# Two thirds of the attention probabilities transposed by VectorE and two trips through memory instead of by TensorE

## The chip, the cores and the metric

The kernel runs on one core of one Trainium2 chip. The metric is the device time of one execution in microseconds (us); the lower, the better.

## What is computed

A decoder trunk of two layers in fp32, for one sequence of 256 tokens with 1024 channels. Each layer adds half a SwiGLU FFN (inner width 2816), a mixer, and half of another FFN to the stream, each behind an RMSNorm; a last RMSNorm ends it.

```python
for layer in range(DEPTH):
    h = h + 0.5 * swiglu(rms_norm(h, ffn1_norm[layer]), ...)
    hn = rms_norm(h, mix_norm[layer])
    h = h + (ab_mixer(hn, ...) if layer % 2 == 0 else c_mixer(hn, ...))
    h = h + 0.5 * swiglu(rms_norm(h, ffn2_norm[layer]), ...)
return rms_norm(h, final_norm)
```

The mixer of layer 0 (ab) has eight causal attention heads of 64 channels under a fixed mask with weights, beside four groups of a spatial gate that mixes positions by a causal 128x128 matrix. The mixer of layer 1 (c) has 16 heads of 64 channels; at 256 tokens and blocks of 256 its block-sparse attention is plain causal attention. So in both, a head is softmax(q k^T + mask) v over 256 queries and 256 keys. The change concerns one step of that: for the product with v the softmax's probabilities, computed with the queries on the partitions, are needed with the keys on the partitions.

## The kernel before

**fp32 as three passes.** Each product of fp32 matrices is done as three matmuls in the format fp32r (`mm3`, L265 to L268): high part by high part, high by low, low by high. An operand is split by a ScalarE (ACT) copy to fp32r, which is the high part, and a VectorE (DVE) subtraction, which gives the low part (`split`, L271).

**The stream of weights.** The weights come as chunks of up to 1 MB by SyncE's (SP's) DMA queue into three raw buffers (L139, `Stream`), and are split into four buffers each of high and low parts (`whi` by ACT at L172, `wlo` by DVE at L173). `pump` loads and splits ahead as buffers come free; TensorE (PE) consumes the chunks in a fixed order. `hold` and `release` keep splits back around some steps of the ab mixer; `release` places them behind given instructions.

**Phases.** ffn, ab_mixer, ffn, ffn, c_mixer, ffn. In a mixer the projections to q, k and v (and to the gate's u and its norm in ab) run tile by tile: a tile of 128 output channels is 24 matmuls of 256 columns, half a block of v 12 of 512 columns. Each such piece is a step, and after it `Slots.step` emits the attention's pieces that are registered for this step number. The output projection, `project`, consumes `mix`, a pair of heads at a time, and has steps as well.

**A head's pieces.** `scores` makes the raw scores on PE (L700, L701), the masked minimum on DVE (L704), the exponential on ACT (L707), the reciprocal of the sum on DVE (L710) and the scaling on GpSimd (POOL; for the last heads on DVE, L714). The result is `pr`: 128 query partitions by 384 columns, since of the first 128 queries only 128 keys count. `turn` transposes it in three 128x128 blocks on PE (L723) into a PSUM bank and splits that into `pth` and `ptl` (L271). `weighted` multiplies a pair of heads with v (three matmuls of 512 columns and three of 256) and splits the result into `mixh` and `mixl`. `put_q`, `put_k` and `put_v` evict the projections' tiles (L659 to L685, L820, L821), `mixing` is the spatial gate (L859 to L868).

**Order.** Each engine executes its instructions in one fixed order, written at build time: a scheduler sorts the emitted instructions, and `tc.issue_after(x)` keeps what is emitted under it behind instruction x. Waits between engines are semaphores.

Of the kernel before, what the change touches and what calls it, by code (L numbers as in the profile page):

```python
# [10 lines left out]
F32 = mybir.dt.float32  # L11
# [4 lines left out]
S = 256  # L16
# [19 lines left out]
LINE, SHIFT = 64, 16  # L36
EDGE, GAP = 56, 240

# [76 lines left out]
class Stream:  # L115
# [31 lines left out]
    def split_parts(self):  # L147
        j = self.split
        nc = self.nc
        nk, w, _, shift, cuts, reset = self.specs[j]  # L150
        raw = self.raws.pop(j)
        his, los = (p.tile([128, CH + LINE], F32R, name=m) for p, m in ((self.hi_pool, "whi"), (self.lo_pool, "wlo")))

        h = w // 2
        far = nk * w - reset * h + RESHIFT // LINE * LINE + RESHIFT

        def at(k):
            return int(k * w) - reset * h + shift

        def part(t, k):  # L160
            if k >= reset:
                return t[:, at(k) : at(k) + w]
            return Halves(*(t[:, a : a + h] for a in (far + k * h, shift + k * h)))

        self.parts[j] = tuple([part(t, k) for k in range(nk)] for t in (his, los))

        def split(a, r):
            n = r.free_size()
            hi, lo = his[:, a : a + n], los[:, a : a + n]
            if len(r.shape) == 3:  # L170
                hi, lo = (t.rearrange("p (k c) -> p k c", k=reset) for t in (hi, lo))
            nc.scalar.activation(hi, r, AF.Copy)  # L172
            nc.vector.tensor_sub(lo, r, hi.bitcast(F32))  # L173
# [51 lines left out]
def trunk(ctx: ExitStack, tc: tile.TileContext, a, out):  # L225
# [419 lines left out]
    def make_attention(mp, mask_cols, nheads, v, mix, rows=False):  # L645

        qs, ks, probs, pts = {}, {}, {}, {}
        pairs, flying = (4, 5) if rows else (2, 4)
        seconds = [mp.tile([128, 2 * S + LINE], F32R, name=f"ql{i}") for i in range(pairs)]
# [7 lines left out]
        def scaled(bk):  # L657
            t = mp.tile([128, S], F32, name="qk", bufs=3)
            nc.vector.tensor_mul(t, bk[:, :S], norm["row"])  # L659
            return t  # L660
# [30 lines left out]
        def scores(h):  # L691
            q, ql = qs.pop(h)
            k = ks.pop(h)
            sc = bank()
            pr = mp.tile([128, 384], F32, name="pr", bufs=flying)
            nm = wk.tile([128, 2], F32, name="nm")
# [12 lines left out]
            rl = wk.tile([128, 2], F32, name="rl")  # L709
            nc.vector.reciprocal(rl, l)  # L710
            for b, (c0, n) in enumerate(((0, 128), (128, 256))):
# [27 lines left out]
        return put_q, put_k, scores, turn, weighted  # L739

# [83 lines left out]
    def ab_mixer(phase):  # L824
        with tc.tile_pool(name="mp", bufs=1) as mp:
# [3 lines left out]
            uT = mp.tile([128, 4, S], F32, name="uT")  # L829
            put_q, put_k, scores, turn, weighted = make_attention(mp, slice(0, 384), 8, v, mix)  # L830

# [63 lines left out]
    def c_mixer(phase):  # L895
        with tc.tile_pool(name="mp", bufs=1) as mp:
            mix = mix_tiles(mp)
            v = v_tiles(mp, D)
            put_q, put_k, scores, turn, weighted = make_attention(mp, slice(384, 768), 16, v, mix, True)
# [90 lines left out]
```

## Time and profile before

| what | value |
|---|---|
| median of 3 runs | 937.71 us |
| the three runs | 937.48, 937.71, 942.17 us |
| profiled execution | 937.01 us |
| its span on the core | 935.3 us |
| PE busy in the span | 927.7 us (99%) |
| DVE busy | 612.1 us (65%) |
| ACT busy | 499.2 us (53%) |
| POOL busy | 83.0 us (9%) |
| HBM | 173.72 MB read, 2.10 MB written |

The span is the part of the execution that the profile covers from its first to its last instruction. A row of a group reads: line, engine, operation, out<-in with shapes, count, then busy us and mean ns of one, then the engine's idle time just before and what ended it. In a timeline the first two numbers are the start in us from the span's start and the duration in us; the duration of a PE matmul contains a pipeline latency, so the distance from start to start is its cost. A row of a stretch (window) has the busy time of PE, PE's weight loads, DVE, ACT and POOL, with counts, then the granted clock, the share of the DMA engines and the GB/s. A row of DMA issues has size and median us from issue to landing.

### The profile page before, as it was taken

What the parts mean: (1) busy time and instruction counts of PE and PEld (TensorE: products, weight loads), DVE (VectorE), ACT (ScalarE), POOL (GpSimd) and SP (SyncE); (2) the same over time, 40 slices, a digit from 0 to 9 for tenths busy, and PEclk for the clock granted to TensorE, in tenths of its full rate; (3) what the DMA queues carried; (4) which work ended last, traced back from release to release, by engine and by line L of the source; (5) the groups of instructions that cost most, each with busy time, mean ns of one, the idle gap of its engine ahead of it and who ended that gap; (6) DMA issues with size and microseconds to landing.
All of it is one profiled execution on the core that took longest, in us unless ns stands there. A gap on an engine that the chain in (4) does not pass through costs nothing.

```text
span 935.3 us, 18101 instructions
## 1 busy us (share of the span) xinstructions
PE 927.7 (99%) x7655; PEld 907.4 (97%) x7655; DVE 612.1 (65%) x892; ACT 499.2 (53%) x782; POOL 83.0 (9%) x114
## 2 busy tenths in 40 slices
PE   9999999999999999999999999999999999999997
PEld 9999999999999999999999999999999999999886
DVE  7866556676888666555756665567787786656543
ACT  7744444468667454444454544456786665445431
POOL 0000000034210000000000000002574000000000
PEclk9999999999999999999999999999999999999999
DMA  8755554665336555555555555556543377555521
GB/s 320 281 212 181 189 194 162 223 222 180 136 136 226 188 211 188 183 175 206 204 184 200 204 180 170 203 184 220 177 139 136 137 243 269 186 188 210 190 90 46
DMA packets 28305, 176.99 MB, mean 189 GB/s; under 512 B 3264, under 2 KB 4672, under 8 KB 9152
## 3 DMA queue, kind: packets, MB, share of 16 engines
q1 hardware_dynamic: 26928, 173.65, 52.5%
q10 hardware_dynamic: 1296, 2.18, 0.7%
q8 instruction: 60, 0.98, 0.4%
q14 instruction: 21, 0.17, 0.0%
HBM read 173.72 MB, written 2.10 MB: 188 GB/s over the span
## 4 chain that ended last, share of the span: by engine, by line
PE 98%; issue 1%; DMA 0%; ACT 0%; SPq 0%; DVE 0%; POOLq 0%; POOL 0%
PE bank L266 30%; PE bank L267 30%; PE bank L268 30%; PE bank L567 2%; PE bank L571 2%; PE bank L568 2%; PE bank L723 1%; PE bank L700 1%; PE bank L701 1%; DMA x<-in_x 0%; PE bank L343 0%; PE bank L859 0%; PE bank L361 0%; PE bank L455 0%; PE bank L456 0%
## 5 line engine op out<-in xcount | busy, mean ns | idle before, releaser
L172 ACT ACTIVATE whi<-raw 128x1024 fp32r<-128x1024 f32 (+3 forms) x352 | 330.5, 985 | 350.1 <-issue 282.9
L173 DVE TENSOR_TENSOR wlo<-raw,whi 128x1024 fp32r<-128x1024 f32 (+3 forms) x352 | 389.6, 1141 | 126.7 <-ACT whi L172 125.8
L266 PE MATMUL bank<-xTh,whi 128*128 128x256 f32 x1616 | 447.9, 277 | 0.0
L267 PE MATMUL bank<-xTl,whi 128*128 128x256 f32 x1616 | 446.7, 276 | 0.0
L268 PE MATMUL bank<-xTh,wlo 128*128 128x256 f32 x1616 | 446.6, 276 | 0.0
L267 PEld LDWEIGHTS bank<-xTl,whi 128*128 128x128 f32 x1616 | 303.5, 188 | 0.2
L266 PEld LDWEIGHTS bank<-xTh,whi 128*128 128x128 f32 x1616 | 303.5, 188 | 0.0
L268 PEld LDWEIGHTS bank<-xTh,wlo 128*128 128x128 f32 x1616 | 303.5, 188 | 0.0
L267 PE MATMUL bank<-hTl,whi 128*128 128x256 f32 x528 | 145.8, 276 | 0.0
L266 PE MATMUL bank<-hTh,whi 128*128 128x256 f32 x528 | 145.8, 276 | 0.0
L268 PE MATMUL bank<-hTh,wlo 128*128 128x256 f32 x528 | 145.8, 276 | 0.0
L266 PEld LDWEIGHTS bank<-hTh,whi 128*128 128x128 f32 x528 | 99.1, 188 | 0.0
L268 PEld LDWEIGHTS bank<-hTh,wlo 128*128 128x128 f32 x528 | 99.1, 188 | 0.0
L267 PEld LDWEIGHTS bank<-hTl,whi 128*128 128x128 f32 x528 | 99.1, 188 | 0.0
L506 DVE TENSOR_TENSOR hm<-gs,bank 128x512 f32<-128x512 f32 x44 | 30.1, 687 | 77.7 <-PE bank L268 77.3
L503 DVE TENSOR_TENSOR gs<-bank,row 128x512 f32<-128x512 f32 x44 | 30.0, 689 | 47.8 <-PE bank L268 47.8
L266 PE MATMUL bank<-mixh,whi 128*128 128x256 f32 x128 | 35.3, 281 | 0.0
L267 PE MATMUL bank<-mixl,whi 128*128 128x256 f32 x128 | 35.1, 277 | 0.0
L268 PE MATMUL bank<-mixh,wlo 128*128 128x256 f32 x128 | 35.0, 277 | 0.0
L714 POOL TENSOR_SCALAR pr<-pr,rl 128x128 f32<-128x128 f32 (+1 forms) x36 | 30.8, 870 | 25.2 <-DVE rl L710 14.1
L653 POOL MEMSET ql<- 64x256 f32 x12 | 3.7, 307 | 328.7 <-ACT whi L172 170.3
L567 PE MATMUL bank<-whi,hTh 128*128 128x512 f32 x80 | 31.1, 389 | 0.0
(134 smaller groups left out, 877.4 us busy)
## 6 DMA issues: line engine op xcount, KB each, us to landing
raw<-in_weights SPq DMA_DIRECT2D x149, 1024.0 KB, 4.9
raw<-in_weights SPq DMA_DIRECT2D x12, 768.0 KB, 4.4
raw<-in_weights SPq DMA_DIRECT2D x6, 512.0 KB, 6.5
x<-in_x SPq DMA_DIRECT2D x4, 264.0 KB, 4.0
raw<-in_weights SPq DMA_DIRECT2D x4, 256.0 KB, 4.3
away<-xn SPq DMA_DIRECT2D x2, 512.0 KB, 5.5
xr<-away SPq DMA_DIRECT2D x8, 128.0 KB, 5.7
fg<-in_final_norm ACTq DMA_DIRECT2D x1, 512.0 KB, 3.7
```

The costliest lines, as they stand in the source:

```text
L172: nc.scalar.activation(hi, r, AF.Copy)
L173: nc.vector.tensor_sub(lo, r, hi.bitcast(F32))
L266: nc.tensor.matmul(p, sh, mh, start=start, stop=False)
L267: nc.tensor.matmul(p, sh, ml, start=False, stop=False)
L268: nc.tensor.matmul(p, sl, mh, start=False, stop=stop)
L503: nc.vector.tensor_mul(g, both(pg), twice(norm["row"]))
L506: nc.vector.tensor_mul(hm, g, both(pu))
L567: nc.tensor.matmul(banks[t, h], sh, w[0][kw][:, cs], start=k == 0, stop=False)
L568: nc.tensor.matmul(banks[t, h], sh, w[1][kw][:, cs], start=False, stop=False)
L571: nc.tensor.matmul(banks[t, h], sl, w[0][kw][:, cs], start=False, stop=k == FT - 1)
L700: nc.tensor.matmul(sc[:, b * S : (b + 1) * S], q[:, bs], k, start=True, stop=False)
L714: share = engine.tensor_scalar(pr[:, cs], pr[:, cs], rl[:, b : b + 1], None, op0=ALU.mult)
```

## The change

For the first four of the eight heads of ab and the first twelve of the sixteen of c, in groups of four, the transposition leaves PE. `tilt`, two steps behind the scores, transposes `pr` (128x384) on DVE in blocks of 32x32 into `turned`; it stands behind the latest reciprocal, or for the fourth head of a group behind the latest weight split. `send` writes the group to memory by four DMAs on SP, one for each 32 partitions; `fetch` reads it back by four more into `ptl`, with the blocks where the full transpose has them. `part` then splits: two ACT copies of 128x768 from `ptl` to `pth`, and two DVE subtractions in place; it is issued behind the latest weight split on both engines. `weighted` of these heads stands in later slots. The last four heads of each mixer go on as before, by `turn` on PE, though `pr` lies in `turned`.

`pth` and `ptl` now hold four heads in one buffer each, with the heads' columns interleaved in 32s, so `weighted` reads its moving operand in runs of 64 elements and `mix` is written accordingly. `pr` goes from 4 (ab) and 5 (c) buffers to 3, `qk` from 3 to 2, and the padding `GAP` from 240 to 112 elements. In c four of the sixteen scores stand one step earlier.

```diff
-EDGE, GAP = 56, 240
+EDGE, GAP = 56, 112
...
-            nc.scalar.activation(hi, r, AF.Copy)
-            nc.vector.tensor_sub(lo, r, hi.bitcast(F32))
+            self.last = nc.scalar.activation(hi, r, AF.Copy), nc.vector.tensor_sub(lo, r, hi.bitcast(F32))
...
-        qs, ks, probs, pts = {}, {}, {}, {}
-        pairs, flying = (4, 5) if rows else (2, 4)
+        qs, ks, probs, pts, sent = {}, {}, {}, {}, {}
+        pairs = 4 if rows else 2
+        late = nheads - 4
         seconds = [mp.tile([128, 2 * S + LINE], F32R, name=f"ql{i}") for i in range(pairs)]
...
-            t = mp.tile([128, S], F32, name="qk", bufs=3)
+            t = mp.tile([128, S], F32, name="qk", bufs=2)
...
-            pr = mp.tile([128, 384], F32, name="pr", bufs=flying)
+            if h < late:
+                pr = mp.tile([128, 384], F32, name="pr", bufs=3)
+            else:
+                if h == late:
+                    probs["turned"] = turned_tile()
+                pr = probs["turned"].rearrange("p m j h r -> p (m j h r)")[:, h % 4 * 384 : (h % 4 + 1) * 384]
...
-            nc.vector.reciprocal(rl, l)
+            probs["behind"] = nc.vector.reciprocal(rl, l)
...
+        def turned_tile():
+            return mp.tile([128, 3, 4, 4, 32], F32, name="turned")
+
+        def tilt(h):
+
+            if h % 4 == 0:
+                probs["turned"] = turned_tile()
+            turned = probs["turned"]
+            behind = st.last[1] if h % 4 == 3 else probs["behind"]
+            with tc.issue_after(behind.ins):
+                nc.vector.transpose(turned[:, :, :, h % 4].rearrange("p m j r -> p (m j) r"),
+                                    probs.pop(h).rearrange("p (b c) -> p b c", c=32))
+
+        def send(g):
+            sent[g] = dram.tile([32, 12, 4, 128], F32, name=f"sent{nheads}{g}")
+            for i in range(4):
+                nc.sync.dma_start(sent[g][:, :, i],
+                                  probs["turned"][i * 32 : (i + 1) * 32].rearrange("c m j h r -> c (m j) (h r)"))
+
+        def fetch(g):
+
+            src = sent.pop(g).rearrange("c (m j) i f -> j c m (i f)", j=4)
+            pts[g] = parts = part_tiles()
+            for j in range(4):
+                nc.sync.dma_start(parts[1][j * 32 : (j + 1) * 32].bitcast(F32).rearrange("p (m i) h r -> p m (i h r)", m=3),
+                                  src[j])
+
+        def part(g):
+
+            with tc.issue_after(st.last[0].ins), tc.issue_after(st.last[1].ins):
+                for q in range(2):
+                    hi, lo = (t[:, q * 6 : (q + 1) * 6] for t in pts[g])
+                    nc.scalar.activation(hi, lo.bitcast(F32), AF.Copy)
+                    nc.vector.tensor_sub(lo, lo.bitcast(F32), hi.bitcast(F32))
+
+        def part_tiles():
+
+            return [mp.tile([128, 12, 4, 32], F32R, name=n) for n in ("pth", "ptl")]
+
         def turn(h):
-            p, j = divmod(h, 2)
+            g, j = divmod(h, 4)
             pr = probs.pop(h)
             tp = bank()
             for i in range(3):
                 nc.tensor.transpose(tp[:, i * 128 : (i + 1) * 128], pr[:, i * 128 : (i + 1) * 128], ident)
             if j == 0:
-                pts[p] = [mp.tile([128, 2, 384], F32R, name=n, bufs=2) for n in ("pth", "ptl")]
-            return split(pts[p][0][:, j, :], pts[p][1][:, j, :], tp[:, :384])
+                pts[g] = part_tiles()
+            return split(*(t[:, :, j] for t in pts[g]), tp[:, :384].rearrange("p (b r) -> p b r", r=32))
 
         def weighted(p):
-            o = bank().rearrange("p (j c) -> p j c", j=2)
-            pth, ptl = pts.pop(p)
+            o = bank()
+            hs = slice(p % 2 * 2, p % 2 * 2 + 2)
             vs = slice(p * 128, (p + 1) * 128)
-            mm3(o, v[0][:, 0, vs], v[1][:, 0, vs], pth[:, :, :256], ptl[:, :, :256], True, False)
-            mm3(o[:, :, 128:], v[0][:, 1, vs], v[1][:, 1, vs], pth[:, :, 256:], ptl[:, :, 256:], False, True)
+            for b, (q, n) in enumerate(((slice(0, 8), 0), (slice(8, 12), 256))):
+                mm3(o[:, n:], v[0][:, b, vs], v[1][:, b, vs],
+                    *(t[:, q, hs].rearrange("p b h r -> p b (h r)") for t in pts[p // 2]), b == 0, b == 1)
             for j in range(2):
                 r = slice(j * 64, j * 64 + 64)
-                done = split(mix[0][r, p], mix[1][r, p], o[r, j, :].rearrange("p (t c) -> p t c", t=NT))
+                done = split(*(m[r, p].rearrange("p t (i r) -> p (t i) r", r=32) for m in mix),
+                             o[r].rearrange("p (b h r) -> p b h r", h=2, r=32)[:, :, j])
             return done
 
...
-            slots.at((10, 10, 12, 12, 22), turn)
+            slots.at((8, 9, 10, 12), tilt)
+            slots.at((12,), send)
+            slots.at((13,), fetch)
+            slots.at((16,), part)
+            slots.at((22,), lambda _: turn(4))
             slots.at((22,), lambda _: st.release(tc, turn(5), True))
             slots.at((23, 23), lambda i: turn(6 + i))
-            slots.at((13, 14, 24), weighted)
+            slots.at((17, 18, 24), weighted)
...
-            slots.at((5, 6, 7, 8, 12, 13, 14, 15, 16, 17, 18, 19, 24, 24, 25, 25), scores)
-            slots.at((9, 9, 11, 11, 16, 16, 18, 18, 20, 20, 22, 22, 26, 26, 27, 27), turn)
-            slots.at((11, 13, 18, 20, 22, 24, 28, 29), weighted)
+            slots.at((5, 6, 7, 8, 11, 12, 13, 14, 16, 17, 18, 19, 24, 24, 25, 25), scores)
+            slots.at((7, 8, 9, 10, 13, 14, 15, 16, 18, 19, 20, 21), tilt)
+            slots.at((10, 16, 21), send)
+            slots.at((15, 21, 25), part)
+            slots.at((16, 17, 22, 22, 26, 26, 28, 29), weighted)
+            slots.at((12, 18, 22), fetch)
+            slots.at((26, 26, 27, 27), lambda i: turn(12 + i))
```

More of the change, by code (lines that the diff above doesn't have):

```diff
@@ L724, in turn @@
             if j == 0:
-                pts[p] = [mp.tile([128, 2, 384], F32R, name=n, bufs=2) for n in ("pth", "ptl")]
-            return split(pts[p][0][:, j, :], pts[p][1][:, j, :], tp[:, :384])
+                pts[g] = part_tiles()
+            return split(*(t[:, :, j] for t in pts[g]), tp[:, :384].rearrange("p (b r) -> p b r", r=32))
         def weighted(p):
-            o = bank().rearrange("p (j c) -> p j c", j=2)
-            pth, ptl = pts.pop(p)
+            o = bank()
+            hs = slice(p % 2 * 2, p % 2 * 2 + 2)
             vs = slice(p * 128, (p + 1) * 128)
-            mm3(o, v[0][:, 0, vs], v[1][:, 0, vs], pth[:, :, :256], ptl[:, :, :256], True, False)
-            mm3(o[:, :, 128:], v[0][:, 1, vs], v[1][:, 1, vs], pth[:, :, 256:], ptl[:, :, 256:], False, True)
+            for b, (q, n) in enumerate(((slice(0, 8), 0), (slice(8, 12), 256))):
+                mm3(o[:, n:], v[0][:, b, vs], v[1][:, b, vs],
+                    *(t[:, q, hs].rearrange("p b h r -> p b (h r)") for t in pts[p // 2]), b == 0, b == 1)
             for j in range(2):
                 r = slice(j * 64, j * 64 + 64)
-                done = split(mix[0][r, p], mix[1][r, p], o[r, j, :].rearrange("p (t c) -> p t c", t=NT))
+                done = split(*(m[r, p].rearrange("p t (i r) -> p (t i) r", r=32) for m in mix),
+                             o[r].rearrange("p (b h r) -> p b h r", h=2, r=32)[:, :, j])
             return done
-        return put_q, put_k, scores, turn, weighted
+        return put_q, put_k, scores, tilt, send, fetch, part, turn, weighted
     def mix_tiles(mp):
@@ L829, in ab_mixer @@
             uT = mp.tile([128, 4, S], F32, name="uT")
-            put_q, put_k, scores, turn, weighted = make_attention(mp, slice(0, 384), 8, v, mix)
+            put_q, put_k, scores, tilt, send, fetch, part, turn, weighted = make_attention(mp, slice(0, 384), 8, v, mix)
             vgain = mp.tile([128, 512], F32, name="vgain")
@@ L898, in c_mixer @@
             v = v_tiles(mp, D)
-            put_q, put_k, scores, turn, weighted = make_attention(mp, slice(384, 768), 16, v, mix, True)
+            put_q, put_k, scores, tilt, send, fetch, part, turn, weighted = make_attention(mp, slice(384, 768), 16, v, mix, True)
             slots = Slots()
-            slots.at((5, 6, 7, 8, 12, 13, 14, 15, 16, 17, 18, 19, 24, 24, 25, 25), scores)
-            slots.at((9, 9, 11, 11, 16, 16, 18, 18, 20, 20, 22, 22, 26, 26, 27, 27), turn)
-            slots.at((11, 13, 18, 20, 22, 24, 28, 29), weighted)
+            slots.at((5, 6, 7, 8, 11, 12, 13, 14, 16, 17, 18, 19, 24, 24, 25, 25), scores)
[5 more added lines that the diff above has]
+            slots.at((26, 26, 27, 27), lambda i: turn(12 + i))
             step = slots.step
```

## The prediction

> **What bounds the kernel now.** I read the page first (engine table, clock slices, chain), then the groups of instructions by form, then the timeline of single engines around the attention of both mixers, and last the order in which the changed kernel's instructions stand on each engine. The page:
>
> ```profile
> span 935.3 us, 18101 instructions
> PE 927.7 (99%) x7655; PEld 907.4 (97%) x7655; DVE 612.1 (65%) x892; ACT 499.2 (53%) x782; POOL 83.0 (9%) x114
> ...
> PEclk9999999999999999999999999999999999999999
> ...
> PE 98%; issue 1%; DMA 0%; ACT 0%; SPq 0%; DVE 0%; POOLq 0%; POOL 0%
> ```
>
> PE is busy 99% of the span and is 98% of the chain that ended last. The view of waits has a single line for it, ahead of the first matmul:
>
> ```profile
> PE bank L442 <- DVE warm L435: 1.1, 1, 1.1
> ```
>
> So two rules hold: PE work that goes comes off the time one for one, and each microsecond that PE waits is added one for one, since nothing later has slack in which to recover it. The profiled execution took 937.01 us, 1.7 us more than its span; the median of the runs is 937.71. I sum against 937.0.
>
> **What is removed from PE.** 48 of 72 transposes.
>
> ```profile
> L723 PE MATMUL bank<-ident,pr 128*128 128x128 f32 x72 | 9.9, 273 | 0.0
> ...
> 219.44 0.39 PE L268 MATMUL bank<-whi,xTl 128*128 128x512 f32 x1
> 219.68 0.82 PE L723 MATMUL bank<-ident,pr 128*128 128x128 f32 x6
> 220.25 0.48 PE L266 MATMUL bank<-whi,xTh 128*128 128x512 f32 x1
> 220.56 0.39 PE L267 MATMUL bank<-wlo,xTh 128*128 128x512 f32 x1
> ```
>
> The 273 ns is latency; matmuls overlap. What counts is start to start: six transposes occupy 219.68 to 220.25, 0.57 us, and the matmul after them takes 0.31 to its successor where its neighbours (219.44 to 219.68) take 0.23 or 0.24, so 0.08 to 0.1 more. Six cost 0.66 us, one 0.11. 48 x 0.11 = **5.4 us off** (1.3 in ab, 4.0 in c). All other columns that PE processes stay.
>
> The Trainium skill (VectorE: DVE Perf Modes, The three transpose paths) gives 390 ns for a 128x128 transpose on TensorE against 311 ns on VectorE in 32x32 blocks only, in bf16. By 390 ns, 48 would be 18.7 us (an estimate from that page); the timeline's start to start shows 0.11 us, so the measurement decides.
>
> **What DVE, ACT and the DMA queues get.** Rows for this and for the waits below:
>
> ```profile
> L172 ACT ACTIVATE whi<-raw 128x1024 fp32r<-128x1024 f32 x272 | 275.2, 1053 | 299.2 <-issue 237.8 <-PE bank L267 36.7 <-PE bank L571 13.6
> ...
> L172 ACT ACTIVATE whi<-raw 128x768 fp32r<-128x768 f32 x26 | 20.7, 839 | 39.6 <-issue 39.6
> L271 ACT ACTIVATE pth<-bank 128x384 fp32r<-128x384 f32 x24 | 10.5, 486 | 0.5 <-PE bank L723 0.2
> L867 ACT ACTIVATE mixh<-tmp 128x256 fp32r<-128x256 f32 x4 | 1.7, 418 | 3.0 <-DVE tmp L865 3.0
> L820 ACT ACTIVATE vth<-bank,rstd 128x512 fp32r<-128x512 f32 x6 | 4.1, 679 | 0.6 <-PE bank L268 0.6
> ...
> L173 DVE TENSOR_TENSOR wlo<-raw,whi 128x1024 fp32r<-128x1024 f32 x272 | 324.3, 1225 | 91.5 <-ACT whi L172 91.1
> L173 DVE TENSOR_TENSOR wlo<-raw,whi 128x768 fp32r<-128x768 f32 x26 | 23.8, 954 | 26.1 <-ACT whi L172 25.8
> L271 DVE TENSOR_TENSOR ptl<-bank,pth 128x384 fp32r<-128x384 f32 x24 | 12.3, 547 | 2.1 <-ACT pth L271 2.0
> L659 DVE TENSOR_TENSOR qk<-bank,row 128x256 f32<-128x256 f32 x16 | 6.4, 418 | 0.5 <-PE bank L268 0.3
> L821 DVE SCALAR_TENSOR_TENSOR vtl<-bank,rstd,vth 128x512 fp32r<-128x512 f32 x6 | 4.4, 737 | 0.0
> L491 DVE STREAM_TRANSPOSE xn<-x 128x128 f32<-128x128 f32 x16 | 3.6, 278 | 0.0
> ...
> 193.00:275.00 82.00, 81.88 (x608) 77.09 (x607) 62.78 (x139) 57.29 (x130) 26.92 (x32) 1.00 0.46 159
> 620.00:737.00 117.00, 117.00 (x911) 112.11 (x911) 89.89 (x197) 83.75 (x181) 49.16 (x65) 1.00 0.48 171
> ...
> away<-xn SPq DMA_DIRECT2D x2, 512.0 KB, 5.5
> xr<-away SPq DMA_DIRECT2D x8, 128.0 KB, 5.7
> ```
>
> DVE loses 16 subtractions of 547 ns (8.8 us). It gains 8 of 128x768 (nearest 954 ns: 7.6 us) and 16 tilts. A 128x128 block transpose is 278 ns, and elementwise rows go from 0.42 us at 256 columns to 1.2 at 1024, so I take 0.55 us for 384 columns (between 0.28 and 3 x 278 = 0.83): 8.8 us. Net +7.6 us, in two stretches where DVE has 19 and 27 us idle (the two windows). ACT loses 16 x 486 and gains 8 x 839, about -1 us. The weight splits stand on these engines; the cover is their lead: the split that starts at 735.38 on DVE (row below) feeds matmuls that begin at 753.7. I cost this at nothing; without that cover it would be up to 7.6 us.
>
> Each group makes four sends to memory and four fetches on SP, among the weight loads. With the analogues, 5.5 + 5.7 = 11.2 us for the round trip; a step is 24 matmuls of 0.11 us (243.53 to 243.64 below), 2.7 us. The send stands five (ab) to six steps ahead of the first matmul that needs the data, 13.5 us or more. I cost the landing at nothing too. If the eight transfers landed one behind another, as bad as twice 11.2, a group would be late by 22.4 - 13.5 = 9 us: kept for the rivals.
>
> `weighted` now reads its moving operand in runs of 64 elements. No row of before shows such runs; its operand there is in runs of 128 and 256. I take 0; the twelve units remaining in PE's order as many columns as before, a price of a tenth would be about 1 us.
>
> **What the order forces: the new waits.** This decides. Engines work in order. `part` (two ACT copies to pth, then two DVE subtractions to ptl) has to be issued behind the last weight split. In the changed kernel's order that puts it behind operations that themselves wait for the matmuls right in front of the `weighted` that needs it, so PE reaches `weighted` before `part` can start. What is queued behind `part` on ACT and DVE (mix evictions, k copies, later splits) waits with it; PE, which waits anyway, is the only one that pays. How fast such chains start and run:
>
> ```profile
> 243.53 0.28 PE L268 MATMUL bank<-xTh,wlo 128*128 128x256 f32 x1
> 243.64 0.61 PE L859 MATMUL bank<-wsT,vn 128*128 128x128 f32 x4
> 244.00 0.37 PE L266 MATMUL bank<-xTh,whi 128*128 128x256 f32 x1
> ...
> 734.09 0.28 PE L268 MATMUL bank<-mixh,wlo 128*128 128x256 f32 x1
> ...
> 734.29 2.01 ACT L172 ACTIVATE whi<-raw 128x1024 fp32r<-128x1024 f32 x2 [0.52 <-PE bank L267]
> ...
> 735.38 2.36 DVE L173 TENSOR_TENSOR wlo<-raw,whi 128x1024 fp32r<-128x1024 f32 x2 [0.76 <-ACT whi L172]
> ...
> 753.66 0.28 PE L266 MATMUL bank<-xTh,whi 128*128 128x256 f32 x1
> ...
> 243.05 0.85 ACT L672 ACTIVATE q<-qk 64x256 fp32r<-64x256 f32 x2 [1.11 <-DVE qk L659]
> ...
> 248.43 1.16 DVE L673 TENSOR_TENSOR ql<-qk,q 64x256 fp32r<-64x256 f32 x2
> 249.62 0.42 DVE L865 TENSOR_TENSOR tmp<-tmp,uT 128x256 f32<-128x256 f32 x1
> ```
>
> A weight split that waits for PE's last use of a chunk starts 0.1 us after PE's next slot; its DVE half trails ACT by 1.1 us. The two halves of `part` are taken as 0.84 us each on ACT (1.6 as an overlapped pair) and 0.95 on DVE. The four places, t = 0 being the last matmul awaited:
>
> - **c, heads 8 to 11.** ACT: both halves of a split waiting for the projection's last use of its chunk (2.0, done at 2.1), the two pth copies (3.7). PE's slot for `weighted` is at 0.2: 3.5 us of waiting. Then two matmuls against pth (0.5) cover PE to 4.2. DVE: split to 3.5, ptl at 4.5 and 5.4: 1.2 more. **4.7 us.** Behind it, the last heads' transposes and the projection wait for mix and for banks: 0.5 more.
> - **c, heads 4 to 7.** DVE qk (0.42) behind the k tile's last matmul, two k copies on ACT (0.85, done at 1.4), pth at 3.0; PE waits 2.9. Two matmuls cover to 3.5; ptl at 4.1. **3.6 us.**
> - **c, heads 0 to 3.** ACT vth (0.68) behind the v block's last matmul, pth at 2.4; slot at 0.2: 2.2. Three matmuls of 0.23 cover to 3.2; DVE vtl, then ptl at 3.5: 0.4. **2.7 us.**
> - **ab, heads 0 to 3.** `weighted` follows the last mixing directly. ACT: half a split (1.05, to 1.1), q copies (1.95), the other half (2.95), mixh from tmp. tmp's product stands on DVE behind half a split (2.35) and two ql (1.16, to 3.5), so ends at 3.9; mixh at 4.3, pth at 5.9. The mixing takes 0.36 (243.64 to 244.00), so the slot is at 0.4: 5.5. Five short matmuls cover 0.7; DVE's second split half (to 5.1), ptl at 6.0 and 6.9: 0.4. **5.9 us.**
>
> Sum 4.7 + 0.5 + 3.6 + 2.7 + 5.9 = 17.4 us. In before PE has no such wait: it is busy 81.88 of 82 and 117.00 of 117 us in the two windows.
>
> Time: 937.0 - 5.4 + 17.4 = **949.0 us**. The per-place error is some 0.5 us, as the idle state of ACT and DVE on arrival is a guess: if they arrive late, each place grows.
>
> **Rivals.**
>
> 1. *The waits do not form: faster.* What stands ahead of `part` on ACT and DVE is done by the time PE gets to `weighted`, since PE itself is held up there by a few microseconds of other work, or because I have misread which matmul is awaited. Then only the transposes count: 937.0 - 5.4 = 931.6. For it: ACT and DVE are idle 30% and 23% of the ab window, 28% and 23% of c's. Against it: they would wait for PE's own last matmuls, so idleness does not help. It decides if the waits sum to less than 5.4 us, under a third of mine. Chance 0.10.
>
> 2. *The waits are half as long.* The chains overlap more than the pairs quoted, the second halves above all: 8.7 us in place of 17.4, 937.0 - 5.4 + 8.7 = 940.3. Against it: copy and subtraction are taken at durations of rows. Chance 0.10, of which 0.06 within the bound of no change.
>
> 3. *PE's clock falls in the long waits.* The granted clock is full in all 40 slices, and the view of waits knows no PE wait after the start, so the trace cannot show what a gap of 5.5 us does. If PE came back at half rate for about one step, 2.7 us would be added per fall: in ab and in c's longest, up to 5.4 us, 954.4. The Trainium skill (TensorE: Matmul & The Clock Gate, What's actually happening) says that one idle window of about 3.4 us throttles PE to half rate until it has been busy as long; no run here shows it yet. Chance 0.20.
>
> 4. *The fetches come late.* They decide from a round trip of 13.5 us on; at the bound of 9 us for one group, 958.0. For it: SP has weight loads in between, and the fetch waits for the send's landing. Chance 0.10.
>
> The main case, 944 to 953, keeps 0.50.
>
> **How the numbers follow.** About 0.5%, 4.7 us, is what a measurement can tell from no change: faster is below 933.0, slower above 942.4. Faster: rival 1, 0.10. Same: that part of rival 2, 0.06. Slower: the rest, 0.04 + 0.20 + 0.10 + 0.50 = 0.84. The range leaves out rival 1 and what lies beyond one late group, with 0.85 inside: 938 to 958.
>
> **What would show it.** Right: 24 transposes at start to start 0.11; pth and ptl (128x768, 8 each) as releasers of PE waits of 5.9, 2.7, 3.6 and 4.7 us, 17 in sum; DVE's busy time up 7 to 8 us; tilts near 0.55 us. Wrong: PE without gaps at `weighted` (rival 1); gaps whose releaser is ptl's DMA (rival 4); a granted clock below 1.00 and matmuls over 0.114 apart behind a gap (rival 3); `weighted`'s six matmuls longer than 1.0 us start to start from runs of 64.

## The result, and the profile after

The changed kernel takes 966.81 us (median of 970.30, 966.81, 966.57, 966.81), the kernel before 937.6 on the same chip: a ratio of 1.031 [1.027, 1.035], 29 us slower. Forecast were 949.0 us and a range to 958. The direction was right, the size was not: 17.8 us are missing. The profiled execution is the one of 970.30; what sets it apart from the other three, some 4 us, is in the last section. The views of the changed kernel are all of that execution.

The page of the changed kernel:

```profile
span 968.6 us, 18051 instructions
...
PE 936.9 (97%) x7607; PEld 912.5 (94%) x7607; DVE 619.4 (64%) x900; ACT 499.3 (52%) x774; POOL 83.2 (9%) x114
...
PEclk9999999999899999999999999999998899999999
...
PE 88%; DVE 4%; ACT 4%; issue 2%; POOL 1%; DMA 1%; SPq 0%; POOLq 0%; DVEq 0%; ACTq 0%
...
sent<-turned SPq DMA_DIRECT2D x16, 192.0 KB, 3.8
ptl<-sent SPq DMA_DIRECT2D x16, 192.0 KB, 5.7
```

PE, 98% of the chain before, is 88% of it now: DVE, ACT, POOL and the DMAs have got onto it. The clock row, full in all 40 slices before, has an 8 in slice 11 (ab) and in slices 31 and 32 (c). And PE is busy for 9.2 us longer than before, although 48 transposes went.

Its view of waits, PE's lines (waited in all, times, the longest):

```profile
PE bank L265 <- ACT pth L755: 20.5, 4, 8.3
PE bank L266 <- DVE ptl L756: 1.2, 3, 0.5
PE bank L905 <- DVE vn L899: 1.2, 1, 1.2
PE bank L705 <- POOL k L685: 1.2, 1, 1.2
PE bank L441 <- DVE warm L434: 1.1, 1, 1.1
```

The last line stood in before too. The other four are new, 24.1 us. The view counts from the modelled end of the matmul in front; from start to start, less a matmul's normal spacing, the same waits come to 26.0 us. The four on pth, in PE's timeline:

```profile
241.93 0.60 PE L905 MATMUL bank<-wsT,vn 128*128 128x128 f32 x4
250.87 0.80 PE L265 MATMUL bank<-pth,vth 128*128 128x512 f32 x1 [8.34 <-ACT pth L755]
251.46 0.41 PE L265 MATMUL bank<-xTh,whi 128*128 128x256 f32 x1
...
707.45 0.50 PE L265 MATMUL bank<-pth,vth 128*128 128x512 f32 x1 [2.25 <-ACT pth L755]
...
733.63 0.80 PE L265 MATMUL bank<-pth,vth 128*128 128x512 f32 x1 [6.46 <-ACT pth L755]
...
757.64 0.80 PE L265 MATMUL bank<-pth,vth 128*128 128x512 f32 x1 [3.45 <-ACT pth L755]
```

In ab the last mixing's matmuls begin at 241.93 and `weighted` 8.9 us later. Behind the gap a matmul of 512 columns takes 0.59 us to its successor (250.87 to 251.46), where 0.23 is normal. The windows of one microsecond behind the gaps (the granted clock is the third figure from the end) say why:

```profile
250.00:251.00 1.00, 0.13 (x1) 0.13 (x1) 0.92 (x2) 0.81 (x2) 0.62 (x1) 0.50 0.00 0
254.00:255.00 1.00, 1.00 (x9) 1.00 (x8) 0.34 (x1) 0.38 (x1) 0.00 (x0) 0.73 0.20 74
255.00:256.00 1.00, 1.00 (x11) 1.00 (x10) 0.51 (x2) 0.38 (x1) 0.00 (x0) 1.00 0.00 0
708.00:709.00 1.00, 0.52 (x2) 0.34 (x2) 0.60 (x1) 0.00 (x0) 0.00 (x0) 0.75 0.87 311
711.00:712.00 1.00, 1.00 (x4) 0.74 (x4) 0.56 (x2) 0.38 (x1) 0.00 (x0) 0.54 0.25 67
739.00:740.00 1.00, 1.00 (x10) 1.00 (x9) 0.52 (x2) 0.38 (x1) 0.00 (x0) 0.89 0.33 84
763.00:764.00 1.00, 1.00 (x10) 1.00 (x9) 0.50 (x2) 0.73 (x3) 0.00 (x0) 0.94 0.00 0
```

PE's clock is at one half behind each of the four gaps: to 254.5, from 708.5 to 711.9, to 739.2 and to 763.1 (a row of 0.73 is 0.54 us at half and the rest at full clock). From the ends of the gaps that is 3.7, 3.4, 5.6 and 5.5 us at half clock, 18.2 in all. In 1.5 us of it PE waits once more, for ptl; half of the rest is lost, 8.3 us.

The account from the forecast's terms: 937.0 - 5.4 + 26.0 + 8.3 = 965.9. With the some 4 us of the last section that is 970, and the profiled execution took 970.30. The other three executions, at the median of 966.8, were not profiled. Their mean granted clock was 0.982 to 0.984 against 0.986 here, so they had more half clock, and how their time divides is not known.

### The profile page after: what moved, and what is told of

It is laid out like the page before. It is cut to its first block, busy times and chain, and to the rows that moved or that the text cites. A ratio compares the mean times of both kernels' runs of the same rounds, so it can differ in the third digit from the quotient of the medians.

```text
span 968.6 us, 18051 instructions
## 1 busy us (share of the span) xinstructions
PE 936.9 (97%) x7607; PEld 912.5 (94%) x7607; DVE 619.4 (64%) x900; ACT 499.3 (52%) x774; POOL 83.2 (9%) x114
## 4 chain that ended last, share of the span: by engine, by line
PE 88%; DVE 4%; ACT 4%; issue 2%; POOL 1%; DMA 1%; SPq 0%; POOLq 0%; DVEq 0%; ACTq 0%
PE bank L266 27%; PE bank L267 27%; PE bank L265 27%; DVE wlo L172 2%; PE bank L570 2%; PE bank L567 2%; PE bank L566 2%; ACT whi L172 2%; ACT pr L712 1%; DVE ptl L756 1%; DMA x<-in_x 1%; PE bank L705 0%; DVE ql L673 0%; PE bank L706 0%; ACT pth L755 0%
## 5 line engine op out<-in xcount | busy, mean ns | idle before, releaser
L567 PE MATMUL bank<-wlo,hTh 128*128 128x512 f32 x80 | 31.2, 389 | 0.0
```

The source lines that it names most:

```text
L567: nc.tensor.matmul(banks[t, h], sh, w[1][kw][:, cs], start=False, stop=False)
```

## The experiments

Five explanations compete for the 17.8 us beyond the forecast, and for the 29 in all. **A**: `part` is late because of its place, behind whatever ACT and DVE have in hand. **C**: the tilts load DVE and delay what `part` waits for. **D**: the clock falls in the waits. **F**: the round trip through memory is late. **P**: the saved transposes bring nothing, as PE then only arrives earlier at its wait. Times before were 937.5 to 937.8 in all comparisons.

**part_first.** In the changed kernel, the splits and evictions emitted after `part` are kept behind it on ACT and DVE. PE's order is the same.

```diff
+                    st.parted = (nc.scalar.activation(...), nc.vector.tensor_sub(...))
...
+            with st.behind_part(tc):   # around split of a chunk, put_q, put_k, put_v, mixing's evictions
```

> The order of PE's instructions is that of the changed kernel; on ACT and DVE the two copies and subtractions of part now stand ahead of the evictions and weight splits that wait for PE's own last matmuls. Theory A (the place of part in the order makes the waits): the waits for pth and ptl fall from 21.7 us to under 9 (ab from 8.6 to about 5.5, bound by the landing of the fetch at 246.0, the first and last group of c to under 0.5, the middle one from 6.5 to about 2), at most two stretches at half clock are left, time 945 to 952 us. Rival B (the data arrive too late whatever the order): waits and time as they are, 965 to 968. Rival C (DVE and ACT are late from earlier work, tilts above all): the waits shrink by less than a third, 960 to 965.

Measured: 953.93 us, 1.017 [1.014, 1.020]. Its waits, and the start of `part` on ACT in ab:

```profile
PE bank L273 <- ACT pth L773: 10.2, 4, 5.3
PE bank L274 <- DVE ptl L774: 1.2, 3, 0.4
...
246.08 1.58 ACT L773 ACTIVATE pth<-ptl 128x768 fp32r<-128x768 f32 x2 [1.06 <-DMA ptl<-sent]
```

The waits for pth halve; with ptl they are 11.4 us, more than the 9 expected. Each wait of c's first and third groups is under 0.6 us, and the clock no longer falls there. 12.9 us of the 29 came from the place: A stands. What is left has another releaser. In ab ACT now stands idle until the DMA lands at 246.0, 3.8 us past PE's arrival at 242.2. In c's second group the wait is still 4.5 us, and there too ACT waits for the DMA, until 723.0, 2.8 us past PE's arrival at 720.2:

```profile
723.04 1.58 ACT L773 ACTIVATE pth<-ptl 128x768 fp32r<-128x768 f32 x2 [1.55 <-DMA ptl<-sent]
```

Behind the first cause there was a second, F, in two of the four places.

**fill.** In the changed kernel PE gets 60 more matmuls of 512 columns to do where it would idle: 34 in front of ab's first `weighted`, 26 in front of the one of c's second group. Their results are overwritten.

```diff
+            fill = {80: 34, 162: 26}.get(nheads * 10 + p, 0)
+                for _ in range(fill):
+                    st.ahead = nc.tensor.matmul(o, v[0][:, 0, vs], xT["h"][:, :2]..., start=True, stop=True)
```

> In front of the weighted that waits longest in ab and in c, 34 and 26 matmuls of 512 columns are added whose result is overwritten; at 0.228 us each they take 7.8 and 5.9 us, about what PE waits there. Theory D (the granted clock falls because PE idles): behind these two places the clock stays at 1.00 and the matmuls at 0.228 and 0.114 us; the 1.6 and 2.9 us lost there go, and the kernel with 60 more matmuls takes 961 to 963.5 us. Rival E (the matmuls behind the gap are slow for another reason: strided reads, DMA traffic): they stay at 0.43 and 0.21 us, 966 to 968 us or more.

Measured: 964.87 us, 1.029 [1.026, 1.033]. Waits of its first two groups in c (670 to 745 us), then those of the changed kernel in the same stretch:

```profile
PE bank L269 <- ACT pth L759: 2.8, 2, 2.3
```

```profile
PE bank L265 <- ACT pth L755: 8.7, 2, 6.5
```

PE does 60 matmuls more and is not slower. The median lies between the two forecasts, and the four executions spread from 963.28 to 968.70 us, so the time alone decides nothing; the clock does. The half clock behind the second group's place is gone, in ab it is 3.4 us in place of 6.8, and at the places without filling it is as before. The price of the clock is separate from the wait, as D says.

**tilt_small.** In the changed kernel the tilt transposes only 32 of the 384 columns; the other probabilities sent are zeros, so the products of these heads are not computed.

```diff
-                nc.vector.transpose(turned[:, :, :, h % 4]..., probs.pop(h)...)
+                nc.vector.transpose(turned[:, 2, 3, h % 4], probs.pop(h)[:, 352:])
```

> Each tilt transposes one 32x32 block per partition group (32 columns) in place of twelve (384); the rest of the tile that is sent holds zeros, so the probabilities of twelve heads in c and four in ab are left out. All waits and transfers stay. Theory C (the tilts' 8.8 us on DVE and the waits in front of them make DVE late): the wait in ab falls from 8.3 to about 6, that of c's middle group from 6.5 to about 3.5, the new waits for vn and k (1.2 each) go; 957 to 961 us. Rival A (order alone): all waits within 1 us of the changed kernel's, 965 to 967 us.

Measured: 967.27 us, 1.031 [1.028, 1.034].

```profile
PE 933.6 (97%) x7607; PEld 909.6 (94%) x7607; DVE 614.9 (64%) x900; ACT 499.4 (52%) x774; POOL 85.9 (9%) x116
...
PE bank L265 <- ACT pth L756: 21.0, 4, 8.3
```

DVE is busy 4.5 us less, about half of what the tilts take (POOL clears the buffer in addition), and the waits are the same. C falls: the time of the tilts is off the path, as the forecast had it. Their place in DVE's order is not tested by this.

**fetch_free.** In the changed kernel the fetches read a memory tile written at the mixer's start, so they need not wait for the sends; those of ab and of c's first two groups stand one or two steps earlier. `weighted` of these heads thus computes with other data.

```diff
-            src = sent.pop(g).rearrange(...)
+            src = stale.rearrange(...)
...
-            slots.at((13,), fetch)          # ab
+            slots.at((11,), fetch)
-            slots.at((12, 18, 22), fetch)   # c
+            slots.at((10, 17, 22), fetch)
```

> The fetch reads another tile in memory, written at the start of the mixer, so it need not wait for the send and is issued one or two steps earlier in ab and in the first group of c; the sends stay, and the probabilities of the transposed heads are left out. In the order of this kernel part then stands earlier in ab and the first group of c, and where it was in the other two. Theory F (the trip through memory is what pushes part behind PE's own matmuls): the waits of ab (9.1 us) and of c's first group (3.1) vanish with their half-clock stretches (1.6 and 1.8), the other two stay: 949 to 953 us. Rival C (DVE is late anyway): at least half of ab's wait stays, 956 to 962 us.

Measured: 958.14 us, 1.021 [1.019, 1.024].

```profile
PE bank L265 <- ACT pth L758: 11.6, 2, 7.2
PE bank L266 <- DVE ptl L759: 4.7, 2, 3.7
```

8.7 us less. ab's wait for pth and that of c's first group are gone: the copies start as soon as ACT is free, in ab at 239.87, ahead of the mixing's evictions. But ptl is then the last to come in ab (3.7 us), and c's later two groups wait a little longer than before (11.6 us in place of 9.9). F is a part of it, in ab and the first group of c; there the scheduler's order on ACT moved too, so this run doesn't part F from A.

**first_later.** part_first, with ab's first two `weighted` at steps 20 and 21 in place of 17 and 18, and those of c's second group and the third group's fetch at 23 in place of 22.

```diff
-            slots.at((17, 18, 24), weighted)
+            slots.at((20, 21, 24), weighted)
...
-            slots.at((16, 17, 22, 22, 26, 26, 28, 29), weighted)
+            slots.at((16, 17, 23, 23, 26, 26, 28, 29), weighted)
```

> As the kernel with part first, and weighted stands later: in ab at steps 20 and 21 (17 and 18 before), for c's middle group at 23 (22), with its next fetch at 23. Theory A (what is left is the landing of the fetch, which a later weighted hides): ab's wait for pth (5.3 us with 3.4 to 6.8 us at half clock) goes, that of c's middle group falls from 4.4 to about 2; 939 to 943 us. Rival I (ACT and DVE cannot keep up with PE in these stretches, so the wait only moves to the new place): 947 to 954 us.

Measured: 952.70 us, 1.015 [1.013, 1.018]; the profiled execution 953.72. All of PE's waits between 190 and 290 us:

```profile
PE bank L924 <- DVE vn L918: 1.2, 1, 1.2
PE bank L785 <- POOL turned L737: 0.6, 1, 0.6
```

With steps between fetch and use, no wait for pth is left in ab and 3.4 us in all. Yet the time hardly moves, far from the 939 to 943 us of theory A. Some waits stay (the 3.4 us in c, 2.1 for ptl, 1.2 each for vn and k, and two falls of the clock). And in the profiled execution the matmuls between 297 and 470 us ran 0.118 apart instead of 0.113 at full granted clock, some 6.6 us (173 us x 0.0045 / 0.1178). That rhythm belongs to the last section.

**best2** and **best3.** Attempts at a better version: part_first with the scores of head 4 back at step 12, ab's mixing at 16, 17, 17, 18 and its `weighted` at 20 and 21, c's first two groups later.

```diff
-            slots.at((15, 16, 16, 17), mixing)
+            slots.at((16, 17, 17, 18), mixing)
...
-            slots.at((5, 6, 7, 8, 11, 12, ...), scores)
+            slots.at((5, 6, 7, 8, 12, 12, ...), scores)
-            slots.at((15, 21, 25), part)                             # best3: unchanged
+            slots.at((15, 21, 26), part)
-            slots.at((16, 17, 22, 22, 26, 26, 28, 29), weighted)
+            slots.at((17, 17, 24, 24, 26, 26, 28, 29), weighted)     # best3: 23, 23
-            slots.at((12, 18, 22), fetch)
+            slots.at((12, 18, 24), fetch)                            # best3: 23
```

> As the one before, with the remaining waits addressed too: the mixing steps one later (16, 17, 17, 18), the scores of c's fifth head at step 12 as in the kernel before the change, c's first two weighted at 17, the middle group's at 24 with its fetch, the last part at 26. Theory A: the waits for vn and k (1.2 each) and c's first two groups' go, some 2 us stay at c's last group; against 5.4 us saved in transposes: 933 to 937 us, faster than the kernel before by up to 4 us. Rival I: the waits move on to c's last group, which has nothing behind it to fill PE: 939 to 946 us.

> As best2, with c's middle group at step 23, its fetch at 23 and the last part at 25. Theory A: 1 to 2 us of wait at the middle group, less at the last: 934 to 939 us. Rival I: 940 to 946 us.

Measured: best2 953.47 us, 1.017 [1.015, 1.019]; best3 950.10 us, 1.013 [1.011, 1.015]. Both lie above the forecasts of either theory. The waits for vn and, in best3, for k are gone. Others took their place: in best2 5.4 us for another k and 3.2 us for pth, in best3 4.3 and 2.5 us for pth; both wait 1.8 us for mixl in ab. best3 is the fastest version of the whole change that ran; it has not got back to before.

**ab_late.** Only ab is changed, with its `weighted` at 20 and 21; c and the padding are as before.

```diff
-EDGE, GAP = 56, 112
+EDGE, GAP = 56, 240
...
-            slots.at((17, 18, 24), weighted)
+            slots.at((20, 21, 24), weighted)
...
+            put_q, put_k, scores, turn, weighted = make_attention_before(mp, slice(384, 768), 16, v, mix, True)
```

> Only ab has the tilt and the trip through memory, for its four heads, with weighted at steps 20 and 21; c is that of the kernel before the change, and so is the padding. Part is not forced ahead. Theory A: 24 of the 48 us of place are not touched; 12 transposes less are worth 1.3 us, the wait for vn costs 1.2, and pth, late by 2.8 us in the changed kernel, is hidden by three steps (8.2 us): 936.5 to 939 us. Rival I (ACT and DVE late in ab whatever the place): 941 to 946 us.

Measured: 952.47 us, 1.012 [1.008, 1.016], but in two groups: 940.41, then 952.35 to 952.79 four times, and 947.01 once. The profiled one is of the upper group, with waits of 1.3, 1.1 and 0.7 us for pth, vn and k, no half clock, and matmuls 0.118 apart from 297 to 665 us. (The expectation of gap_short, below, says from 258 on; between 272 and 296 us the spacing was 0.113.)

**ab_late2.** ab_late with the first mixing at 16 and both `weighted` at 22.

```diff
-            slots.at((15, 16, 16, 17), mixing)
+            slots.at((16, 16, 16, 17), mixing)
...
-            slots.at((20, 21, 24), weighted)
+            slots.at((22, 22, 24), weighted)
```

> Only ab is changed, as in ab_late, with the first mixing one step later (16) and weighted at step 22: the waits for vn (1.1), pth (1.3) and k (0.7) should go. Theory A: without a wait there is no slow rhythm either: 936.3 to 937.5 us, just faster than the kernel before. Rival I: the waits move to another place, 939 to 953 us.

Measured: 944.49 us, 1.008 [1.006, 1.009]. The waits for pth and vn are gone; in their place are 2.9 us for k and 1.8 us for mixh, and one fall of the clock of 3.4 us, as rival I has it. Every order tried in ab left a wait there, at its old place or at a new one.

**gap_short** and **gap_long.** The kernel before with one artificial wait in ab: PE waits for a chain of ACT copies of a PE result, 2 or 9 of them. Apart from two transposes of a constant, PE's work is the same.

```diff
+                    nc.tensor.transpose(b[:, :128], ident, ident)
+                t = mp.tile([128, 128], F32, name="stall")
+                nc.scalar.activation(t, b[:, :128], AF.Copy)
+                for _ in range(n):                               # 1, 8
+                    nc.scalar.activation(t, t, AF.Copy)
+                st.behind = nc.tensor.transpose(b[:, 128:256], t, ident)
...
+            slots.at((14,), lambda _: gap(1))                    # gap_long: gap(8)
```

> The kernel before the change, with one wait put into ab on purpose: behind the second weighted PE transposes a constant, ACT copies the result twice, and PE needs that copy before it goes on; nothing else is changed. The wait should be 1 to 1.4 us. Theory R (a wait of PE, however short, can leave its matmuls at 0.118 instead of 0.113 us from start to start until a later wait, as in the profiled run of the changed kernel from 780 us on and in ab_late from 258 to 665 us): in some or all executions 6 to 16 us are added, 938.5 to 954 us with a wide spread. Rival S (a wait costs what it lasts): 938.6 to 939.4 us in every execution.

> The same with nine copies in place of two: a wait of 3 to 4.5 us at one place. Theory D (PE's clock falls in a wait of over about 2.4 us and comes back only after a whole multiple of 3.41 us): a stretch of 3.4 or 6.8 us at half clock is seen, 1.7 or 3.4 us lost on top of the wait; 942 to 945.5 us without the slow rhythm, up to 15 us more with it. Rival S: 940.5 to 942 us.

Measured: gap_long 946.54 us, 1.010 [1.008, 1.011]; gap_short 942.10, 1.009 [1.005, 1.013], in two groups: 940.15 to 942.11 in seven executions, 953.38 to 954.43 in five. The wait and the clock behind it, gap_long:

```profile
PE bank L882 <- ACT stall L881: 6.8, 1, 6.8
...
241.00:242.00 1.00, 0.87 (x4) 0.87 (x5) 0.00 (x0) 0.08 (x1) 0.00 (x0) 0.50 0.14 57
244.00:245.00 1.00, 1.00 (x9) 1.00 (x9) 0.00 (x0) 0.00 (x0) 0.00 (x0) 0.87 0.00 0
```

and gap_short, in an execution of the upper group:

```profile
PE bank L882 <- ACT stall L881: 2.8, 1, 2.8
...
236.00:237.00 1.00, 0.00 (x0) 0.00 (x0) 1.00 (x2) 0.88 (x3) 0.00 (x0) 1.00 0.00 0
238.00:239.00 1.00, 1.00 (x7) 1.00 (x7) 0.44 (x3) 0.80 (x2) 0.00 (x0) 0.50 1.11 156
```

The waits came out about twice as long as intended. gap_long: PE resumes at 241.13 and has half clock to 244.3: 7.0 of waiting (start to start) and 1.6 for the clock make 8.6, and the time is 9.0 longer. So a wait alone, with nothing of the change in it, costs its length and the half clock behind it: D by itself. gap_short: 3.0 and 1.7 make 4.7, and the lower group, which was not profiled, is 2.6 to 4.6 longer. The two executions of 940.15 and 940.19 us have a mean granted clock of 0.999, as high as any of the kernel before; the other five, 0.997 to 0.998. So the same wait seems to bring the fall in some executions and not in others.

**idle_turn.** The changed kernel, and PE transposes a constant 48 times more, where the transposes stood before; nobody uses the results.

```diff
+                nc.tensor.transpose(tp[:, i * 128 : (i + 1) * 128], ident, ident)
...
+            slots.at((10, 10, 12, 12), idle)                                  # ab
+            slots.at((9, 9, 11, 11, 16, 16, 18, 18, 20, 20, 22, 22), idle)    # c
```

> The changed kernel with the 48 transposes put back on PE in the steps where they stood before the change, of a constant and with no use of the result: PE has its 5.4 us of work back, ACT, DVE and the queues are unchanged. Theory P (without that work PE is ahead of ACT and DVE and only waits longer; the waits end when ACT and DVE are done): the waits for vn, k and pth shrink by what PE does in front of them, 966 to 969 us. Rival Q (the chains in front of part begin with PE's own last matmuls, so the work comes on top): 971 to 973 us.

Measured: 966.70 us, 1.031 [1.030, 1.033], against 966.81 without them.

```profile
PE bank L265 <- ACT pth L755: 17.9, 4, 7.3
...
PE bank L705 <- POOL k L685: 0.5, 1, 0.5
```

The waits are shorter (17.9 in place of 20.5, 0.5 in place of 1.2; 4.3 us in all from start to start). 5.4 us of work is put back, and the time is the same within the 1.5 us by which the executions spread: P is shown.

## Why the prediction was wrong in size

Two terms were too small, about equally. The waits were forecast at 17.4 us and measured 26.0, 8.6 more. The clock that falls behind them was a rival and stood in the sum at nothing; it cost 8.3 us. Together that is 16.9 of the 17.8 us missing.

**The first step that failed is "What the order forces".** The mechanism was right: `part` stands behind operations that wait for PE's own matmuls, PE waits for it at four places, in the forecast's order of engines. The sizes are start to start, less the normal spacing, with ptl:

- c, heads 0 to 3: forecast 2.7, measured 3.1. c, heads 8 to 11: forecast 4.7 and 0.5 behind it, measured 4.5. In both the forecast's own chain is what ran: in the second two weight splits, then two pth copies.
- c, heads 4 to 7: forecast 3.6, measured 6.6. ab: forecast 5.9, measured 9.1.
- not forecast: 1.3 for vn and 1.3 for k.

The error is the assumption of t = 0: that ACT, DVE and POOL are free when PE issues the last matmul awaited. It stood in the text as a guess worth half a microsecond ("if they arrive late, each place grows"); in two of four places it was worth 3 us. Heads 4 to 7, the changed kernel's timeline of DVE and ACT; PE's last matmul in front began at 726.89:

```profile
729.41 1.23 DVE L172 TENSOR_TENSOR wlo<-raw,whi 128x1024 fp32r<-128x1024 f32 x1
730.66 0.42 DVE L659 TENSOR_TENSOR qk<-bank,row 128x256 f32<-128x256 f32 x1
...
731.12 0.85 ACT L683 ACTIVATE k<-qk 64x256 fp32r<-64x256 f32 x2 [3.13 <-DVE qk L659]
732.00 1.58 ACT L755 ACTIVATE pth<-ptl 128x768 fp32r<-128x768 f32 x2
```

The forecast started qk right behind the matmul. It started 3.8 us later, as DVE had tilts, ql and two weight splits in hand, almost back to back; from there on qk, k and pth take what was forecast. The length of the tilts was not the reason: in tilt_small qk starts at 730.67, as late as here. In both, the group's last tilt waits for POOL's scaling of pr (to 727.27 here, 727.11 there), and the splits, ql and qk stand behind it. That moving this tilt would free them was not tested. And ab:

```profile
247.29 1.16 DVE L673 TENSOR_TENSOR ql<-qk,q 64x256 fp32r<-64x256 f32 x2
248.47 0.43 DVE L911 TENSOR_TENSOR tmp<-tmp,uT 128x256 f32<-128x256 f32 x1
...
248.93 0.42 ACT L913 ACTIVATE mixh<-tmp 128x256 fp32r<-128x256 f32 x1 [1.00 <-DVE tmp L911]
249.25 1.56 ACT L755 ACTIVATE pth<-ptl 128x768 fp32r<-128x768 f32 x2
```

The product for mixh was forecast to end 3.9 us behind the last mixing's matmuls and ended at 7.0 (248.90 - 241.93), behind the evictions of the mixings before it. Busy shares of 70 to 77% over the whole mixer did not show that: right in front of `weighted`, from 241 to 250 us, DVE had 0.6 us of idle time. And PE came sooner than before, at 241.93 in place of 243.64 for the last mixing, since transposes (1.3 us) and two `weighted` (1.0 us each) had left the stretch ahead: a shorter path of PE alone lengthens its wait by as much.

**"48 x 0.11 = 5.4 us off"** was right per operation (the product is 5.3) and wrong in what it is worth. The 24 left are 0.11 us apart, as forecast, but idle_turn shows that putting 48 back costs nothing, as 4.3 us of the waits go: a saving in front of a wait that another engine ends goes into the wait. The forecast's rule that PE work comes off one for one holds only where PE has no wait behind it.

**The landing, costed at nothing.** In the changed kernel it is hidden behind the later mixh, so this term did no harm to the sum. But part_first shows that ab and c's second group have no room there: with `part` first, the DMA lands 3.8 and 2.8 us past PE's arrival. The round trip was 11.2 us by the rows of other transfers; from the first send's issue to the last fetch's landing it was 14.0 to 20.5 us in the changed kernel. The transfers by themselves were near those rows (2.7 to 4.5 us a send, 3.5 to 6.5 a fetch, for 5.5 and 5.7); the rest is their issue one behind another and the fetches' place in SP's order, up to 6 us after the last send has landed.

**The waits for vn and k, 2.6 us, costed at nothing.** With the transposes put back (idle_turn), the one for vn is gone and the one for k is 0.65 us in place of 1.3: here too PE had only come earlier. Both also vanish in best3, where the scores of head 4 and the mixing stand later.

**The second step that failed is the clock, left out of the sum: rival 3 came true beside the main case.** The chance was 0.20, for two falls at 2.7 us each; all four waits made the clock fall, at 1.6, 1.6, 2.7 and 2.4 us. The price of one was about right, but as a guess: it was the length of a step, which has no part in it. That a wait of 2.4 us is enough was not foreseen. The Trainium skill (TensorE: Matmul & The Clock Gate, What's actually happening) gives one idle window of about 3.4 us. The length of the half clock agrees, 3.4, 6.8 or 10.2 us in every fall looked at; the idle time that brings it was shorter here (last section).

**Right as forecast:** the tilt and the transposes left on PE, in the groups of the changed kernel:

```profile
L733 DVE STREAM_TRANSPOSE turned<-pr 128x384 f32<-128x384 f32 x16 | 8.6, 557 | 0.7 <-POOL pr L719 0.7
...
L767 PE MATMUL bank<-ident,turned 128*128 128x128 f32 x24 | 3.8, 291 | 0.0
```

0.56 us for 0.55; DVE up 7.3 us for 7.6, off the path (tilt_small). The weight splits stayed covered: no PE wait names whi or wlo beyond the start's 0.2 us. Runs of 64 elements cost nothing: at full clock `weighted`'s matmuls are 0.23 and 0.12 apart as before.

## What to carry to other kernels

A saving on the engine that sets the time is worth something only if no wait behind it ends on another engine: look for the next wait before counting it. Time a chain that starts behind the last matmul from where the other engines really stand then, row by row in the last microseconds, not from their busy share. And a wait of PE of over some 2 us should be priced with the half clock behind it, here up to 2.7 us more.

## What the runs showed of the hardware

**The granted clock goes by fixed windows of 3.41 us, and 60% of a window idle is enough.** In the changed kernel's trace the clock changes at 247.71, 254.53, 708.51, 711.92, 732.40, 739.23, 756.29 and 763.12 us. The distances are whole multiples of 3.413 us: 2, 133, 1, 6, 2, 5 and 2 of them. So it is in each of the twelve traces with a fall before the end, but the instants differ from one to the next. If PE's idle time (start to start, less the normal spacing) is summed by these windows, then by this count every window at full clock with 2.05 us or more was followed by half clock, 30 in all without the end of each trace, and none with up to 2.00 us; full clock came back after the first window with no more than some 0.8 us.

That settles what single gaps leave open. A gap of 2.2 us (start to start) lay in one window in best2, 2.3 us of idle time with its neighbours, and the clock fell; in best3 the edge at 251.54 cut it, 1.9 and 1.2 us, and the clock stayed. In fill gaps of 1.0 and 1.5 us fell into one window, 2.1 us, and were enough. And as the window has to end first, the fall can come when PE is back at work: in the changed kernel PE resumes at 707.45 and the clock falls at 708.5. It also fits that gap_short's wait of 3.0 us cost some executions the fall and others not: by these numbers an edge near its middle leaves 1.5 us on either side.

**Two rhythms at full granted clock.** Windows of 50 us in two FFNs of the changed kernel's profile:

```profile
590.00:640.00 50.00, 50.00 (x443) 50.00 (x442) 30.58 (x37) 23.03 (x32) 0.00 (x0) 1.00 0.50 180
830.00:880.00 50.00, 50.00 (x427) 50.00 (x427) 29.24 (x31) 21.61 (x27) 0.00 (x0) 1.00 0.53 183
```

The same kind of matmuls, PE busy throughout, clock 1.00, but 443 against 427 of them: 0.113 or 0.118 us from start to start. The second lasts from 795 us through the FFN and makes the profiled execution some 4 us longer than it would be. In the profiles of gap_short and ab_late it held from 299 and 297 us to 665, where c's mixer begins. At 0.0045 us in each 0.118 that is 14 us, about what lies between the two groups of their times (11 to 14 us). Only executions of the upper groups were profiled, so that the lower ones lack the rhythm is inferred. The long stretch does not begin at a wait: the waits in ab end at 237 and 258 us, and from 272 to 296 us most matmuls stand 0.113 apart. It sets in behind the short matmuls of ident and wide in front of the FFN; behind the same ones the kernel before has nine distances of 0.115 to 0.118 and then 0.113 again. A shorter stretch does set in behind a wait, from 686 to 700 us in the changed kernel, behind the one for k. What decides between the two rhythms was not found.
